# The first quarter of the modulation channel, tile by tile: one layer of a hybrid diffusion backbone on one core

## The chip, the cores and the metric

The kernel runs on one core of one Trainium2 chip. The metric is the device time of one execution in microseconds (us), as the median of several runs. Profiles are of one execution each, taken by the hardware profiler. Engines are named as the profile names them: PE (TensorE; PEld is its weight load), DVE (VectorE), ACT (ScalarE), POOL (GpSimd) and SP (the queue that issues most of the transfers). L12 is line 12 of the kernel.

## The reference, cut to what matters

```python
sh_x, sc_x, gt_x = jnp.split((jax.nn.silu(c) @ w_ada[l] + b_ada[l])[:, None, :], 3, axis=-1)
sh_c, sc_c, gt_c = jnp.split(jax.nn.silu(c_ctx) @ w_ada[l] + b_ada[l], 3, axis=-1)
pc = split_proj(modulate(ctx, sh_c, sc_c), w_in[l], b_in[l])   # h * (1 + scale) + shift, then @ w_in
px = split_proj(modulate(x, sh_x, sc_x), w_in[l], b_in[l])
...                                                            # RG-LRU, differential attention, gMLP
qx = apply_axial_rope(px[2].reshape(B, T, DIFF_HEADS, 2, DIFF_HEAD_DIM), cos, sin)
kx = apply_axial_rope(px[3].reshape(B, T, DIFF_HEADS, 2, DIFF_HEAD_DIM), cos, sin)
kc = pc[3].reshape(B, C, DIFF_HEADS, 2, DIFF_HEAD_DIM)
```

There are 512 latent tokens (x), 256 context tokens (ctx) and 1024 channels; w_ada is 1024 x 3072, w_in 1024 x 12288, all float32. Before anything can be projected, the shift and the scale of every channel must be known: a product of one vector (two of them, for x and for ctx) with two thirds of w_ada.

## The kernel before

The 1024 channels are eight tiles of 128 on the partitions. The head of the kernel (L264 to L457) brings x and ctx from token-major to channel-major, modulates them, and computes the first keys and queries (heads 0 and 1) over the channel tiles as these become ready. It works in four quarters r of two channel tiles each. For quarter 0:

- `to_cm` (L354) transposes x on PE, four 128 x 128 blocks to a channel tile, both tiles of the quarter one after the other.
- `ada_mm` (L332) multiplies the two silu vectors with the quarter's columns of w_ada: for each of 8 row tiles k four products j, each on a 32-column strip of the PE array (`tile_position`), j = 0, 1 for the shift of the two channel tiles, j = 2, 3 for the scale. The compiler makes two PE instructions of each float32 product, so one call is 64 PE instructions. DVE copies the result out of PSUM (adas, L341).
- `ada_cols` (L344) transposes adas on PE (adat), and four DVE instructions add the biases (mods, L351).
- `modulate` (L367) is, for each channel tile, one DVE multiply-add (xm, L372), an ACT copy that rounds to fp32r (the high part, L374) and a subtraction (the low part, L375; on DVE for x, on POOL for ctx).
- `more(name, r)` (L401) adds a quarter's share to a product. `mm3` (L57) makes three PE instructions for each channel tile: high x high (L62), high x low (L63), low x high (L64).

The order of PE is the order of the program, written by hand (`manual_schedule`). The order of DVE, ACT, POOL and SP is chosen by the framework from its own estimate of when each instruction is ready, earlier program lines first. After quarter 0 the loop of L409 runs, on PE: k0, q0, k1, q1 over quarter 0 (24 instructions, 128 x 512), `ada_mm(1)`, kc0, `ada_cols(1)`, and so on for the other quarters, then the values (v).

Transfers go through SP in program order. A weight of w_in for one head (raw, 512 KB, rows of 512 bytes) has three buffers; its rounding is `w_conv` (L118): an ACT copy (L133) and a subtraction (L134) on DVE or POOL. raw 0 is k0's weight, then q0, k1 and q1. The fourth raw needs the buffer of the first. On SP stand, in this order: x of quarter 0 (512 KB, rows of 1 KB), three small rows of vectors, w_ada of quarter 0 (two blocks of 256 columns, shift and scale, in two halves by row tile, 4 x 512 KB, rows of 1 KB), raw 0, raw 1, ctx of quarter 0 (256 KB), x of quarter 1, raw 2, raw 3, w_ada of quarter 1 (2 x 1 MB), and so on.

Of the kernel before, what the change touches and what calls it, by code (L numbers as in the profile page):

```python
# [10 lines left out]
F32 = mybir.dt.float32  # L11
F32R = mybir.dt.float32r  # L12
AF = mybir.ActivationFunctionType
ALU = mybir.AluOpType
PSUM = bass.MemoryType.PSUM

P = 128
D = 1024
KT = 8
T = 512  # L20
TC = 256
# [8 lines left out]
def block_kernel(ctx, tc, x, c, cctx_in, c_ctx, w_ada, b_ada, w_in, b_in, conv_w, conv_b,  # L30
# [3 lines left out]
    nc = tc.nc  # L34
    V, S, G, PE = nc.vector, nc.scalar, nc.gpsimd, nc.tensor
# [11 lines left out]
    def acc_t(name):  # L47
        return acc.tile([P, 512], F32, tag="acc", name=name)

    def big_t(name):  # L50
        return big.tile([P, 1024], F32, tag="big", name=name)
# [5 lines left out]
    def mm3(ps, A, B, asl, bsl, first=True, last=True):  # L57
        n = len(asl)
        for i in range(n):
            ah, al = A[0][asl[i]], A[1][asl[i]]  # L60
            bh, bl = B[0][bsl[i]], B[1][bsl[i]]
            PE.matmul(ps, ah, bh, start=(first and i == 0), stop=False)  # L62
            PE.matmul(ps, ah, bl, start=False, stop=False)  # L63
            PE.matmul(ps, al, bh, start=False, stop=(last and i == n - 1))  # L64

    def proj_cm(ps, W, X, n0, n1, ks=range(KT)):
        mm3(ps, W, X, [np.s_[:, k, :] for k in ks], [np.s_[:, k, n0:n1] for k in ks],
            0 in ks, KT - 1 in ks)
# [13 lines left out]
    reqs, pieces, raws, parts, last = [], [], {}, {}, {}  # L82
# [15 lines left out]
    def w_dma():  # L98
        if state["dma"] >= len(pieces):
            return  # L100
        i, part = pieces[state["dma"]]
        kind, src, c0 = reqs[i][:3]
        if kind == "cm":
            raw = wp.tile([P, KT, P], F32, tag="raw", bufs=3, name=f"raw{i}")
            nc.sync.dma_start(raw, src[:, c0:c0 + P].rearrange("(k p) c -> p k c", p=P))
        elif kind != "tm":
            raw = wp.tile([P, 2, 512], F32, tag="raw", bufs=3, name=f"raw{i}_{part}")
            r0 = 512 * int(kind[1]) + 256 * part
            nc.sync.dma_start(raw, src[r0:r0 + 256, c0:c0 + 512]
                              .rearrange("(k p) c -> p k c", p=P))  # L110
        else:
            raw = wp.tile([P, KT // 2, CW], F32, tag="raw", bufs=3, name=f"raw{i}_{part}")
            nc.sync.dma_start(raw, src[part * 512:part * 512 + 512, c0:c0 + CW]
                              .rearrange("(k p) c -> p k c", p=P))
        raws[state["dma"]] = raw
        state["dma"] += 1
# [54 lines left out]
    for p in range(3):  # L171
        i, ha_, hb_ = 8 * p, 2 * p + 2, 2 * p + 3
# [83 lines left out]
    X = (xh[:, 0], xh[:, 1])  # L256
    chl = gp.tile([P, 2, KT, TC], F32R, tag="c", name="chl")
    C = (chl[:, 0], chl[:, 1])
# [4 lines left out]
    pre = {}  # L263
    with tc.tile_pool(name="hd", bufs=1) as hd:  # L264
        colA = hd.tile([P, P], F32, name="colA")
        mods = hd.tile([P, 4, KT], F32, name="mods")
# [14 lines left out]
        adaw = {}  # L281

        def load_ada(r):
            for c0 in (256 * r, 1024 + 256 * r):
                adaw[c0] = hd.tile([P, KT, 256], F32, tag="ada", bufs=6, name=f"ada{c0}")
            n = KT // 2 if r == 0 else KT
            for k0 in range(0, KT, n):
                for c0 in (256 * r, 1024 + 256 * r):
                    nc.sync.dma_start(adaw[c0][:, k0:k0 + n],
                                      w_ada[0][k0 * P:(k0 + n) * P, c0:c0 + 256]  # L290
                                      .rearrange("(k p) c -> p k c", p=P))

        def load_x(r):
            cs = slice(256 * r, 256 * r + 256)
            nc.sync.dma_start(xtok[:, :, cs], x[0].rearrange("(t p) d -> p t d", p=P)[:, :, cs])

        def load_c(r):
# [1 line left out]
            nc.sync.dma_start(ctok[:, :, cs],  # L299
                              cctx_in[0].rearrange("(t p) d -> p t d", p=P)[:, :, cs])  # L300

        load_x(0)
        load_ada(0)
        w_dma()
        w_dma()
        load_c(0)
        load_x(1)
        w_dma()
# [20 lines left out]

        adas = {}  # L330

        def ada_mm(r):  # L332
            ps = acc_t(f"ada{r}")
            for k in range(KT):
                for j in range(4):
                    c0 = 256 * r + (1024 if j >= 2 else 0)
                    PE.matmul(ps[32 * j:32 * j + 32, 0:P], w32[:, k, :],
                              adaw[c0][:, k, (j % 2) * P:(j % 2) * P + P],
                              start=(k == 0), stop=(k == KT - 1), tile_position=(0, 32 * j))
            sb = hd.tile([P, P], F32, tag="adas", bufs=2, name=f"adas{r}")  # L340
            V.tensor_copy(sb, ps[:, 0:P])  # L341
            adas[r] = sb

        def ada_cols(r):  # L344
            tp = acc_t(f"adat{r}")
            PE.transpose(tp[:, 0:P], adas[r], ident)
            tv = tp[:, 0:P].rearrange("p (t j i) -> p t j i", t=2, j=2)
            for i in range(2):
                for sc in range(2):
                    o = 16 + 8 * sc + 2 * r  # L350
                    V.scalar_tensor_tensor(mods[:, 2 * i + sc, 2 * r:2 * r + 2], tv[:, sc, :, i],  # L351
                                           float(sc), colA[:, o:o + 2], op0=ALU.add, op1=ALU.add)

        def to_cm(r, i):  # L354

            tok, n = ((xtok, T), (ctok, TC))[i]
            tps = [big_t(f"x{i}_0")] if r == 0 else [acc_t(f"x{i}_{r}{j}") for j in range(2 - i)]
            pss = []
            for j in range(2):
                k = 2 * r + j  # L360
                ps = tps[j][:, 0:n] if len(tps) == 2 else tps[0][:, j * n:j * n + n]
                for tt in range(n // P):
                    PE.transpose(ps[:, tt * P:(tt + 1) * P], tok[:, tt, k * P:(k + 1) * P], ident)
                pss.append(ps)
            return pss

        def modulate(r, i, pss):  # L367
            dst, n = ((xh, T), (chl, TC))[i]
            for j in range(2):
                k = 2 * r + j  # L370
                xm = hd.tile([P, n], F32, tag=f"xm{i}", bufs=2, name=f"xm{i}_{k}")
                V.tensor_scalar(xm, pss[j], mods[:, 2 * i + 1, k:k + 1], mods[:, 2 * i, k:k + 1],  # L372
                                op0=ALU.mult, op1=ALU.add)
                S.copy(dst[:, 0, k, :], xm)  # L374
                (V if i == 0 else G).tensor_tensor(dst[:, 1, k, :], xm, f(dst[:, 0, k, :]),  # L375
                                                   ALU.subtract)

        x0 = to_cm(0, 0)
        ada_mm(0)
        ada_cols(0)  # L380
        load_ada(3)
        bi = b_in[0].rearrange("(k p) -> k p", p=P)
        nc.sync.dma_start(rowC[0:96, :], bi)
# [5 lines left out]
        nc.sync.dma_start(rowB[40:56, :], lru_ba[0].rearrange("d (k p) -> (d k) p", p=P))  # L389
        nc.sync.dma_start(rowB[56:72, :], lru_bx[0].rearrange("d (k p) -> (d k) p", p=P))  # L390
        nc.sync.dma_start(rowB[88:96, :], sgu_b[0])
        modulate(0, 0, x0)
        modulate(0, 1, to_cm(0, 1))
        state["use"] = 4

        bks = [big_t(f"pre{i}") for i in range(3)]
        for h in range(2):
            pre["k", h], pre["q", h] = bks[h][:, 0:512], bks[h][:, 512:1024]
            pre["kc", h] = bks[2][:, 512 * h:512 * h + TC]

        def more(name, r):  # L401
            j, h = int(name[-1] == "1") * 2 + int(name[0] == "q"), int(name[-1])
            ks = range(2 * r, 2 * r + 2)
            if name[:2] == "kc":
                proj_cm(pre["kc", h], parts[j], C, 0, TC, ks)
            else:
                proj_cm(pre[name[0], h], parts[j], X, 0, T, ks)

        for r in range(4):  # L409
            more("k0", r)  # L410
            more("q0", r)
            if r == 0:
                state["lo"] = V
                w_conv()
                w_conv()
                state["lo"] = G
                more("k1", r)
                more("q1", r)
            if r == 3:
                more("kc0", r)  # L420
            else:
                ada_mm(r + 1)
            more("kc0" if r == 0 else "k1", r)
            if r < 3:
                ada_cols(r + 1)
                modulate(r + 1, 0, to_cm(r + 1, 0))
            more("kc1" if r == 0 else "q1", r)
            if r < 3:
                modulate(r + 1, 1, to_cm(r + 1, 1))
            if 0 < r < 3:  # L430
                more("kc0", r)
            if r > 0:
                more("kc1", r)
# [20 lines left out]
                               op1=ALU.subtract)  # L454
# [538 lines left out]
    for i in range(9):  # L993
# [3 lines left out]
        if i < 7:  # L997
            W = w_next()
            ps = (acc_t if i else big_t)(f"xa{i + 1}")[:, 0:T]
# [3 lines left out]
            ps = (acc_t if i else big_t)(f"xac{i + 1}")  # L1003
# [121 lines left out]
    for g in range(8):  # L1125
        ps = acc_t(f"gt0{g}")
# [4 lines left out]
        ps = acc_t(f"y0{g}")  # L1131
# [35 lines left out]
    for g in range(8):  # L1167
        ps = acc_t(f"gt2{g}")
# [42 lines left out]
    for g in range(8):  # L1211
        ps = acc_t(f"y2{g}")
# [31 lines left out]
    for half in range(2):  # L1244
        W = w_next()
        for tt in (0, 2, 1, 3):
            ps = bk[tt // 2][:, tt % 2 * 512:tt % 2 * 512 + 512]
# [75 lines left out]
```

## Time and profile before

| | us |
|---|---|
| median of 3 runs | 1012.86 |
| the runs | 1012.6 to 1014.95 |
| the profiled execution, its own time | 1009.53 |
| the span of its profile | 1007.8 |

The profile's views used below are: busy time by stretch (for each stretch its length, then for each engine the busy time and the number of instructions, then the granted clock of PE, the share of the transfer engines and the rate), the timeline of one engine (start, duration or length of a merged group, engine, line, operation, output from inputs; in brackets the idle time before it and what ended it), the chain of work that ended last (start, length, what), and the rate of transfers in slices. Merged groups show the time from the first start to the last end.

### The profile page before, as it was taken

How to read it: one execution, taken by the hardware profiler on the slowest of the kernel's cores; microseconds unless marked ns; L12 is line 12 of the kernel's file. 1: busy time of each engine (PE TensorE's matmuls, PEld its weight loads, DVE VectorE, ACT ScalarE, POOL GpSimd, SP SyncE). 2: the span in 40 equal slices, each digit the busy share in tenths (PEclk: the TensorE clock that was granted, in tenths of full speed). 3: DMA queues.
4: the chain of work that ended last, by engine and by line, in shares of the span. 5: the costliest groups of instructions: out<-in, count | busy, mean ns of one | idle time of the engine just before them, and what ended most of it. 6: DMA issues, size and time to landing. Idle time of an engine off the chain costs nothing.

```text
span 1007.8 us, 13228 instructions
## 1 busy us (share of the span) xinstructions
PE 964.8 (96%) x5239; PEld 816.5 (81%) x5239; DVE 656.2 (65%) x996; ACT 525.7 (52%) x741; POOL 154.8 (15%) x118
## 2 busy tenths in 40 slices
PE   5998899989989999999999999999999999999996
PEld 4796688878878888878888888788888888888886
DVE  4479688787797764788787776378323356425567
ACT  4155846647656797898777886323222133323221
POOL 2143324242342262100000000000000000000002
PEclk7998999989989999999999999999999999999999
DMA  9933130130131122223322323735322432754222
GB/s 309 306 102 89 43 84 22 44 104 21 43 87 39 43 84 63 63 75 93 95 85 83 94 66 112 252 92 154 98 84 84 120 89 73 253 167 144 95 63 84
DMA packets 142996, 103.34 MB, mean 103 GB/s; under 512 B 3629, under 2 KB 133142, under 8 KB 142934
## 3 DMA queue, kind: packets, MB, share of 16 engines
q1 hardware_dynamic: 140790, 95.85, 31.2%
q0 software_dynamic: 2000, 6.56, 2.4%
q8 instruction: 41, 0.67, 0.3%
q14 instruction: 21, 0.17, 0.0%
q10 hardware_dynamic: 144, 0.10, 0.0%
HBM read 94.10 MB, written 4.19 MB: 98 GB/s over the span
## 4 chain that ended last, share of the span: by engine, by line
PE 68%; DVE 17%; ACT 10%; issue 3%; DMA 1%; SPq 1%; POOL 0%; POOLq 0%; ACTq 0%; DVEq 0%
PE y L62 4%; PE y L64 4%; PE y L63 4%; PE gt L62 4%; PE gt L63 4%; PE gt L64 4%; DVE mxn L735 2%; DVE e L750 2%; PE s L725 2%; DVE kd L585 2%; PE out L63 2%; DVE kd L590 1%; PE out L64 1%; PE out L62 1%; PE gc L62 1%
## 5 line engine op out<-in xcount | busy, mean ns | idle before, releaser
L133 ACT CAST w<-raw 128x1024 fp32r<-128x1024 f32 x96 | 99.8, 1045 | 81.9 <-PE y L64 25.3
L134 DVE TENSOR_TENSOR w<-raw,w 128x1024 fp32r<-128x1024 f32 x71 | 86.3, 1220 | 75.4 <-ACT w L133 75.4
L62 PE MATMUL gt<-xhl,w 128*128 128x512 f32 x192 | 75.5, 393 | 0.0
L64 PE MATMUL gt<-xhl,w 128*128 128x512 f32 x192 | 74.8, 390 | 0.0
L63 PE MATMUL gt<-xhl,w 128*128 128x512 f32 x192 | 74.8, 390 | 0.0
L725 PE MATMUL s<-kd,qdq 128*128 128x512 f32 (+1 forms) x256 | 59.0, 371 | 13.1 <-DVE e L750 5.3
L134 POOL TENSOR_TENSOR w<-raw,w 128x1024 fp32r<-128x1024 f32 x25 | 60.9, 2441 | 67.5 <-ACT w L133 67.5
L725 PEld LDWEIGHTS s<-kd,qdq 128*128 128x128 f32 x256 | 44.8, 198 | 24.7 <-issue 12.2
L735 DVE TENSOR_REDUCE mxn<-s 128x1 f32<-128x768 f32 x64 | 58.3, 949 | 8.2 <-PE s L725 8.2
L740 ACT ACTIVATE e<-s,mxn 128x768 f32<-128x768 f32 x32 | 28.8, 900 | 48.5 <-DVE mxn L735 48.5
L1204 POOL PARTITION_BROADCAST grb<-grs x8 | 3.8, 581 | 297.7 <-DVE grs L1201 297.7
L62 PEld LDWEIGHTS gt<-xhl,w 128*128 128x128 f32 x192 | 36.1, 188 | 7.7
L64 PEld LDWEIGHTS gt<-xhl,w 128*128 128x128 f32 x192 | 36.0, 188 | 7.7
L63 PEld LDWEIGHTS gt<-xhl,w 128*128 128x128 f32 x192 | 36.1, 188 | 7.0
L967 POOL DMA_DIRECT2D pa_d<-ha x8 | 4.4, 552 | 220.4 <-DVE ha L966 220.4
L750 DVE SCALAR_TENSOR_TENSOR e<-s,sm,e 128x768 f32<-128x768 f32 x32 | 32.5, 1017 | 6.5 <-ACT e L743 5.7
L54 ACT CAST vh<-v 128x128 fp32r<-128x128 f32 x48 | 12.4, 263 | 42.9 <-PE v L64 19.7
L862 ACT ACT_TABLE_LOAD x25 | 32.1, 1283 | 0.4
L768 DVE TENSOR_TENSOR wtl<-t,wth 128x768 fp32r<-128x768 f32 x32 | 30.3, 949 | 0.6 <-ACT wth L766 0.5
L743 ACT ACTIVATE e<-e,sm 128x768 f32<-128x768 f32 x32 | 29.9, 935 | 0.2 <-DVE sm L742 0.2
L862 ACT ACTIVATE rt<-ri,colB 128x770 f32<-128x770 f32 x32 | 28.1, 904 | 2.5 <-PE ri L64 1.4
L740 ACT ACTIVATE s<-s,mxn 128x768 f32<-128x768 f32 x32 | 27.7, 865 | 0.9 <-DVE mxn L735 0.9
(458 smaller groups left out, 3037.6 us busy)
## 6 DMA issues: line engine op xcount, KB each, us to landing
raw<-in_w_in_dram SPq DMA_DIRECT2D x96, 512.0 KB, 4.0
raw<-in_w_branch_dram SPq DMA_DIRECT2D x24, 512.0 KB, 4.1
ada<-in_w_ada_dram SPq DMA_DIRECT2D x6, 1024.0 KB, 8.5
qdq<-qdq POOLq DMA_DIRECT2D x16, 256.0 KB, 3.2
adg<-in_w_ada_dram SPq DMA_DIRECT2D x8, 512.0 KB, 5.9
raw<-in_w_out_dram SPq DMA_DIRECT2D x8, 512.0 KB, 3.6
xtok<-in_x_dram SPq DMA_DIRECT2D x4, 512.0 KB, 5.6
ada<-in_w_ada_dram SPq DMA_DIRECT2D x4, 512.0 KB, 5.7
```

The source lines that it names most:

```text
L62: PE.matmul(ps, ah, bh, start=(first and i == 0), stop=False)
L63: PE.matmul(ps, ah, bl, start=False, stop=False)
L64: PE.matmul(ps, al, bh, start=False, stop=(last and i == n - 1))
L133: state["hi"] = S.copy(h, raws[j])
L134: state["lo"].tensor_tensor(l, raws[j], f(h), ALU.subtract)
L725: PE.matmul(sp[:, sl], qds[h][:, 2 * m + j, qs], kds[h][:, m, sl], start=(j == 0), stop=(j == 1))
L735: V.tensor_reduce(mxn[:, m:m + 1], sps[m][:, 0:TA], mybir.AxisListType.X, ALU.max, negate=True)
L740: S.activation(e, sps[m][:, 0:TA], AF.Exp, bias=mxn[:, m:m + 1], accum_out=sm[:, m:m + 1])
L743: S.mul(es[i][0], es[i][0], sm[:, 0:1])
L750: V.scalar_tensor_tensor(e0, e1, sm[:, 1:2], e0, op0=ALU.mult, op1=ALU.add)
L768: V.tensor_tensor(wts[h][1][:, :, qs], src, f(wts[h][0][:, :, qs]), ALU.subtract)
L862: order[0] = S.activation(out, in_, fn, **kw)
```

## The change

The w_ada blocks of quarter 0 are loaded in halves by column (128 columns of shift and scale: one channel tile) and no longer in halves by row tile, and x of quarter 0 in two halves of 128 channels. On SP stand now: x of tile 0, w_ada of tile 0, raw 0, x of tile 1, w_ada of tile 1, raw 1, and then everything as before. The pieces have rows of 512 bytes. `ada_mm(0)` and `ada_cols(0)` are called twice, for j = (0, 2) and j = (1, 3); each call of the half makes 32 PE instructions on two strips of the array, a memset and two 32-partition copies in place of one copy, one PE transpose and four small DVE additions. `modulate` of x is called for tile 0, then the three PE instructions of k0 over tile 0 follow, then the second half; the loop's first k0 is cut to tile 1. The two transposed tiles of x of quarter 0 have a PSUM buffer each; `to_cm` still transposes both before the first `ada_mm`.

```diff
         def load_ada(r):
...
-            n = KT // 2 if r == 0 else KT
-            for k0 in range(0, KT, n):
+            for j in range(2 if r == 0 else 1):
+                n = 128 if r == 0 else 256
+                cs = slice(128 * j, 128 * j + n)
+                if r == 0:
+                    load_x(0, cs)
                 for c0 in (256 * r, 1024 + 256 * r):
-                    nc.sync.dma_start(adaw[c0][:, k0:k0 + n],
-                                      w_ada[0][k0 * P:(k0 + n) * P, c0:c0 + 256]
+                    nc.sync.dma_start(adaw[c0][:, :, cs],
+                                      w_ada[0][:, c0 + 128 * j:c0 + 128 * j + n]
                                       .rearrange("(k p) c -> p k c", p=P))
+                if r == 0:
+                    w_dma()
...
-        load_x(0)
         load_ada(0)
-        w_dma()
-        w_dma()
         load_c(0)
...
-        def ada_mm(r):
-            ps = acc_t(f"ada{r}")
+        def ada_mm(r, js=range(4)):
+            ps = acc_t(f"ada{r}_{js[0]}")
             for k in range(KT):
-                for j in range(4):
+                for j in js:
...
-            sb = hd.tile([P, P], F32, tag="adas", bufs=2, name=f"adas{r}")
-            V.tensor_copy(sb, ps[:, 0:P])
+            sb = hd.tile([P, P], F32, tag="adas", bufs=2, name=f"adas{r}_{js[0]}")
+            if len(js) == 4:
+                V.tensor_copy(sb, ps[:, 0:P])
+            else:
+                V.memset(sb, 0.0)
+                for j in js:
+                    V.tensor_copy(sb[32 * j:32 * j + 32, :], ps[32 * j:32 * j + 32, 0:P])
...
-            tps = [big_t(f"x{i}_0")] if r == 0 else [acc_t(f"x{i}_{r}{j}") for j in range(2 - i)]
+            tps = [(big_t if r + i == 0 else acc_t)(f"x{i}_{r}{j}") for j in range(2 - i)]
...
         x0 = to_cm(0, 0)
-        ada_mm(0)
-        ada_cols(0)
...
+        for j in range(2):
+            ada_mm(0, (j, j + 2))
+            ada_cols(0, j, 1)
+            modulate(0, 0, x0, (j,))
+            if j == 0:
+                more("k0", 0, (0,))
...
-        modulate(0, 0, x0)
         modulate(0, 1, to_cm(0, 1))
...
         for r in range(4):
-            more("k0", r)
+            more("k0", r, (1,) if r == 0 else None)
             more("q0", r)
```

## Rows read from the trace of the kernel before

**Rows 1.** The page: busy time, share of the span, instructions.
```profile
PE 964.8 (96%) x5239; PEld 816.5 (81%) x5239; DVE 656.2 (65%) x996; ACT 525.7 (52%) x741; POOL 154.8 (15%) x118
```
**Rows 2.** Busy time by stretch; the last three columns are PE's clock, transfer share, GB/s.
```profile
10.00:13.00 3.00, 1.69 (x41) 1.07 (x34) 0.29 (x1) 0.17 (x1) 0.00 (x0) 1.00 1.14 344
13.00:24.00 11.00, 7.78 (x19) 5.49 (x20) 8.79 (x13) 5.99 (x8) 4.44 (x3) 0.53 1.07 344
24.00:60.00 36.00, 35.42 (x356) 29.11 (x355) 15.34 (x39) 8.36 (x15) 4.32 (x6) 1.00 0.71 226
...
78.00:85.00 7.00, 5.46 (x25) 5.49 (x26) 6.67 (x14) 2.79 (x6) 2.81 (x3) 0.54 0.33 77
```
**Rows 3.** Timeline of PE from the first transposes to quarter 1.
```profile
7.80 2.74 PE L337 MATMUL ada<-ada,w 128*32 128x128 f32 x36
11.46 1.07 PE L337 MATMUL ada<-ada,w 128*32 128x128 f32 x28 [0.92 <-DMA ada<-in_w_ada_dram]
...
15.06 1.11 PE L363 MATMUL x<-ident,ctok 128*128 128x128 f32 x4 [1.81 <-DMA ctok<-in_ctx_dram]
16.69 0.79 PE L62 MATMUL pre<-xhl,w 128*128 128x512 f32 x1 [0.51 <-ACT xhl L374]
18.38 0.80 PE L63 MATMUL pre<-xhl,w 128*128 128x512 f32 x1 [0.90 <-DVE xhl L375]
...
26.41 1.95 PE L337 MATMUL ada<-ada,w 128*32 128x128 f32 x64
...
29.11 0.27 PE L346 MATMUL adat<-ident,adas 128*128 128x128 f32 x1
...
32.10 0.50 PE L63 MATMUL pre<-xhl,w 128*128 128x512 f32 x1 [0.16 <-DVE xhl L375]
```
**Rows 4.** Timeline of DVE in the same stretch.
```profile
12.57 0.29 DVE L341 COPY adas<-ada 128x128 f32<-128x128 f32 x1 [5.34 <-PE ada L337]
13.90 1.22 DVE L134 TENSOR_TENSOR w<-raw,w 128x1024 fp32r<-128x1024 f32 x1 [0.39 <-ACT w L133]
...
15.18 1.52 DVE L372 TENSOR_SCALAR xm<-x,mods 128x512 f32<-128x512 f32 x2
16.66 1.65 DVE L375 TENSOR_TENSOR xhl<-xm,xhl 128x512 fp32r<-128x512 f32 x1
...
28.43 0.29 DVE L341 COPY adas<-ada 128x128 f32<-128x128 f32 x1 [5.65 <-PE ada L337]
...
31.36 0.69 DVE L375 TENSOR_TENSOR xhl<-xm,xhl 128x512 fp32r<-128x512 f32 x1
```
**Rows 5.** Timelines of ACT (first two rows) and of POOL.
```profile
12.82 1.04 ACT L133 CAST w<-raw 128x1024 fp32r<-128x1024 f32 x1 [4.78 <-DMA raw<-in_w_in_dram]
14.28 1.04 ACT L133 CAST w<-raw 128x1024 fp32r<-128x1024 f32 x1 [0.41 <-DMA raw<-in_w_in_dram]
...
15.41 2.36 POOL L134 TENSOR_TENSOR w<-raw,w 128x1024 fp32r<-128x1024 f32 x1 [13.90 <-ACT w L133]
```
**Rows 6.** Transfer rate of the first 60 us, 40 slices of 1.5 us each.
```profile
GB/s 0 200 206 321 378 358 344 348 350 358 358 315 275 386 363 352 355 347 348 348 348 350 379 382 350 353 351 348 331 122 8 209 350 143 9 0 0 0 0 0
```
**Rows 7.** The chain that ended last: product instructions at two clocks, end of the head.
```profile
20.45 0.43 PE pre L64
...
24.41 0.23 PE pre L62
...
57.60 1.06 ACT w4h L133
...
59.82 1.23 DVE w4l L134
...
61.52 1.78 SPq L491
63.36 4.15 DMA rops<-in_rope_s_dram
67.60 1.26 DVE t1k L544
```

More of the change, by code (lines that the diff above doesn't have):

```diff
@@ L285, in load_ada, with load_x @@
                 adaw[c0] = hd.tile([P, KT, 256], F32, tag="ada", bufs=6, name=f"ada{c0}")
-            n = KT // 2 if r == 0 else KT
-            for k0 in range(0, KT, n):
+            for j in range(2 if r == 0 else 1):
[3 more added lines that the diff above has]
+                    load_x(0, cs)
                 for c0 in (256 * r, 1024 + 256 * r):
-                    nc.sync.dma_start(adaw[c0][:, k0:k0 + n],
-                                      w_ada[0][k0 * P:(k0 + n) * P, c0:c0 + 256]
+                    nc.sync.dma_start(adaw[c0][:, :, cs],
+                                      w_ada[0][:, c0 + 128 * j:c0 + 128 * j + n]
                                       .rearrange("(k p) c -> p k c", p=P))
-        def load_x(r):
-            cs = slice(256 * r, 256 * r + 256)
+                if r == 0:
+                    w_dma()
+        def load_x(r, cs=None):
+            if cs is None:
+                cs = slice(256 * r, 256 * r + 256)
             nc.sync.dma_start(xtok[:, :, cs], x[0].rearrange("(t p) d -> p t d", p=P)[:, :, cs])
@@ L339, in ada_mm, with ada_cols @@
                               start=(k == 0), stop=(k == KT - 1), tile_position=(0, 32 * j))
-            sb = hd.tile([P, P], F32, tag="adas", bufs=2, name=f"adas{r}")
-            V.tensor_copy(sb, ps[:, 0:P])
+            sb = hd.tile([P, P], F32, tag="adas", bufs=2, name=f"adas{r}_{js[0]}")
[5 more added lines that the diff above has]
+                    V.tensor_copy(sb[32 * j:32 * j + 32, :], ps[32 * j:32 * j + 32, 0:P])
             adas[r] = sb
-        def ada_cols(r):
-            tp = acc_t(f"adat{r}")
+        def ada_cols(r, j0=0, n=2):
+            tp = acc_t(f"adat{r}_{j0}")
             PE.transpose(tp[:, 0:P], adas[r], ident)
@@ L349, in ada_cols @@
                 for sc in range(2):
-                    o = 16 + 8 * sc + 2 * r
-                    V.scalar_tensor_tensor(mods[:, 2 * i + sc, 2 * r:2 * r + 2], tv[:, sc, :, i],
-                                           float(sc), colA[:, o:o + 2], op0=ALU.add, op1=ALU.add)
+                    k = 2 * r + j0
+                    o = 16 + 8 * sc + k
+                    V.scalar_tensor_tensor(mods[:, 2 * i + sc, k:k + n], tv[:, sc, j0:j0 + n, i],
+                                           float(sc), colA[:, o:o + n], op0=ALU.add, op1=ALU.add)
         def to_cm(r, i):
             tok, n = ((xtok, T), (ctok, TC))[i]
-            tps = [big_t(f"x{i}_0")] if r == 0 else [acc_t(f"x{i}_{r}{j}") for j in range(2 - i)]
+            tps = [(big_t if r + i == 0 else acc_t)(f"x{i}_{r}{j}") for j in range(2 - i)]
             pss = []
@@ L365, in to_cm, with modulate @@
             return pss
-        def modulate(r, i, pss):
+        def modulate(r, i, pss, js=range(2)):
             dst, n = ((xh, T), (chl, TC))[i]
-            for j in range(2):
+            for j in js:
                 k = 2 * r + j
@@ L378, in block_kernel, with more @@
         x0 = to_cm(0, 0)
-        ada_mm(0)
-        ada_cols(0)
+        bks = [big_t(f"pre{i}") for i in range(3)]
+        for h in range(2):
+            pre["k", h], pre["q", h] = bks[h][:, 0:512], bks[h][:, 512:1024]
+            pre["kc", h] = bks[2][:, 512 * h:512 * h + TC]
+        def more(name, r, ks=None):
+            j, h = int(name[-1] == "1") * 2 + int(name[0] == "q"), int(name[-1])
+            ks = ks or range(2 * r, 2 * r + 2)
+            if name[:2] == "kc":
+                proj_cm(pre["kc", h], parts[j], C, 0, TC, ks)
+            else:
+                proj_cm(pre[name[0], h], parts[j], X, 0, T, ks)
+        for j in range(2):
[4 more added lines that the diff above has]
+                more("k0", 0, (0,))
         load_ada(3)
@@ L391, in block_kernel @@
         nc.sync.dma_start(rowB[88:96, :], sgu_b[0])
-        modulate(0, 0, x0)
         modulate(0, 1, to_cm(0, 1))
         state["use"] = 4
[L396 to L407, printed above, removed]
         for r in range(4):
-            more("k0", r)
+            more("k0", r, (1,) if r == 0 else None)
             more("q0", r)
```

## Prediction

> **What bounds the kernel now.** The page's busy times come first [rows 1]: PE is busy 964.8 of 1007.8 us, so a gain in another engine counts only where PE waits for it. The stretches [rows 2] show where it does near the change: from 13 to 24 us PE is busy 7.78 of 11 us at a granted clock of 0.53, that is, nearly all of it at the lower level of 1.2 GHz, and from 24 to 60 us it is busy 35.42 of 36 us at full clock. So the head is paced by transfers and the modulation chain up to about 18 us, and by PE from there to 60. The timelines [rows 3, 4] give the chain: the last w_ada half lands at 11.46, the product ends at 12.53, DVE copies it, PE transposes it, then xm at 15.18, the rounding on ACT, the low part at 16.66, and the first product that needs a low part starts at 18.38. From there PE runs to `ada_mm(1)` at 26.41 with no wait.
>
> What a shift there is worth at the end is read from the chain that ended last [rows 7]: the first rounding of the v weight at 57.60 follows the last quarter's products, the rope tables are issued on SP behind it (61.52), land, and release DVE at 67.60. Every link is timed from PE's end of the head, none from a fixed hour. I therefore count each microsecond by which `ada_mm(1)` moves as one microsecond of the total.
>
> **When the pieces land.** The rate in slices [rows 6] sums to 2.19 MB at 9.0 us, 2.71 at 10.5 and 3.23 at 12. As a test of the method: x and w_ada of quarter 0 with raw 0 are 3.17 MB, which have passed at 11.8, and raw 0's rounding, which waits for that transfer, starts at 12.82 [rows 5]; the lag is 1.0. In the new order tile 1's x is complete after 0.26 + 0.02 + 1.05 + 0.52 + 0.26 = 2.12 MB: passed at 8.8, landed at 9.9. Tile 1's w_ada is complete after 3.17 MB: landed at 12.8, so 1.4 us later than the last w_ada half now, because raw 0 has gone ahead of it. raw 1 stays at 14.3, as the bytes before it are the same. I take the rows of 512 bytes at the old rate: the slices from 10.5 to 15, in which raw 0 and raw 1 pass with such rows, show 344 to 358 GB/s, and those before, with rows of 1 KB, 321 to 378. Were the pieces moved at 344 instead of 358, 2.6 MB would cost 0.3 us.
>
> The other end is fixed too. w_ada of quarter 1 is complete after 7.62 MB, which the slices reach at 24.7; landed at about 25.75. `ada_mm(1)` starts at 26.41 now. **However early the products of quarter 0 come, at most 0.7 us can be won**, since PE's next step waits for that transfer.
>
> **The change part by part.** Removed is the wait of the first product for tile 1's w_ada and for the second xm. Moved are three of the 24 products of k0 to q1. Added is a second pass of adas, adat, mods, and PE has to take it in order. I follow PE through its new program.
>
> (1) Both tiles of x are still transposed ahead of the first `ada_mm`, so this now waits for tile 1's x (9.9), though its own w_ada has landed at about 7.7. Four transposes took 1.11 at the lower clock (ctok) [rows 3]: 11.0.
>
> (2) The half `ada_mm` has 32 instructions on two strips. The whole one took 1.95 for 64 [rows 3], 16 groups of four on four strips, 0.12 a group. No row shows two strips. If the instructions of a strip follow each other and the strips run beside each other, the half has 16 groups as well and costs the full 1.95 at 2.4 GHz, twice that (3.9) at 1.2 GHz. If the instructions are issued one by one at 1.95 / 64 = 0.03 us, it costs 0.98 (1.95 at the lower clock). I take the first reading, since 0.12 is near half of the 0.23 that a product of 512 columns at one pass each takes [rows 7], as 128 columns at two cycles each would. By clock the ends are 0.98 and 3.9. Today's call ran 36 instructions in 2.74 and 28 in 1.07 [rows 3], with one wait between, so partly at the lower level; I take 2.9 for the first half (half the groups at each level): 13.9.
>
> The Trainium skill, page "TensorEngine Tiling (Array Packing)", section "Theoretical Speedup", gives up to 4x for a small dimension of 32 and up to 2x for 64. Two used strips of 32 columns would by that table get 2x at most, so half the work takes the same time, which is the reading taken; no row here shows it.
>
> (3) From the end of `ada_mm` to the product that needs the low part: in quarter 1 from 28.36 to 32.10, 3.74, of which adat stood 0.39 behind other products (adas ends 28.72, adat starts 29.11) [rows 3, 4]. One copy more adds 0.29: 3.6. The memsets go into DVE's idle time before. The low part of tile 0 starts at about 16.8, beside POOL's 2.36 us on the q0 weight, which now starts at 15.41 and hangs on raw 1 as before [rows 5]; the same subtraction beside it took 1.65 against 0.69 alone [rows 4]. I add 0.95: 18.4. At nothing it would be 17.5.
>
> (4) Tile 0's last two products at 0.43 [rows 7]: 19.3. Only now may PE start the second `ada_mm`, whose w_ada has lain there since 12.8. This is the price of putting a product that waits for DVE between the two halves. Second half as the first, 2.9 (again 0.98 to 3.9): 22.2. Chain again 3.6: 25.8. raw 1's rounding and POOL are then past; the k1 and q1 weights' subtractions (1.22 each on DVE) may stand in the way, priced below.
>
> (5) From 25.8, 20 of the 24 products remain. At the higher clock they take 20 x 0.23 = 4.7, at the lower 8.6. Now the clock fell in the gaps before 18.38 and rose only after some 5 us of products without a gap (23 products took 8.03, 0.43 each and then 0.23). With PE idle about 3.5 us ahead of them again, I take 6.5: 32.3.
>
> **Sum.** `ada_mm(1)` starts at 32.3 instead of 26.41: +5.9. With the second half at 3.9 it would be 6.9; with the first two lower bounds of the chain (no POOL contention, higher clock in both halves, 4.7 for the products) 9.9 + 1.1 + 1.95 + 3.6 + 0.9 + 1.95 + 3.6 + 4.7 = 27.7, +1.3. I forecast **+6**. Against the profiled execution (1009.53, span 1007.8) that is 1015.5; the median before is 3.3 higher, 1012.86, so I predict 1018.9. One extra issue on SP (x in two pieces) costs nothing, as transfers there are limited by rate and not by issue. A difference of 0.3%, 3.0 us, is about what a measurement of this kernel can tell from no change.
>
> **The rivals.**
> *Halves at half the price (0.22).* PE issues the strips' instructions one by one and stays at the higher clock: 9.9 + 0.55 + 0.98 + 3.6 + 0.5 + 0.98 + 3.6 = 20.1, then 6.5: 26.6, +0.2, between -0.7 and +3: 1013, within 0.3%. It decides if the group time with two strips falls below about 0.08. For it: no row shows two strips. Against it: PE is idle more than now, and at 1.2 GHz even this reading costs 1.95.
> *Faster (0.04).* The early product fills the gap, PE reaches w_ada of quarter 1 at 25.75 (-0.7), and in addition the later stretch at the lower clock (5.46 us busy at 0.54, 78 to 85 us) [rows 2] falls away, which gives 5.46 / 2 = 2.7: -3.4, 1009.5. Nothing in the change touches that stretch but the hour at which PE arrives.
> *More in the chain (0.16).* The framework already put a 1.22 us weight subtraction (13.90) between PE's transpose and xm [rows 4]. With two chains there are two places for it, and an ACT rounding of 1.04 [rows 5] may stand ahead of xh's: +1.2 to +2.4 on the sum, 1020 to 1021.5. If `ada_mm` for tile 0 waits for both column halves after all (that is, the split does nothing), it starts at 12.8 and not 11.0, +1.8, the same range.
> *Transfers (in the last case's chance).* The Trainium skill, page "DMA: Bandwidth & Descriptors", section "Rules for kernel authors", asks for few transfers of 1 MiB or more, and its fit has about 2.0 us fixed for each; x in two pieces would then bring tile 1's x 2 us later. In the rows such a price doesn't show: with pieces of 256 and 512 KB in the queue the slices stay at 344 to 358 [rows 6].
>
> **How the numbers follow.** The forecast (+3 to +8.5, chance 0.58) and the longer chain (0.16) are slower by over 0.3%: 0.74. Same: 0.22. Faster: 0.04. The likeliest case's own range is 1016 to 1021.5. The range that leaves out two in ten goes lower into the case of cheap halves: 1012.8 to 1021.8.
>
> **What would show it.** Right: the first x transposes of tile 1 near 10 us; 32 L337 instructions taking about 2 us at the higher or 3.9 at the lower clock; the second `ada_mm` starting only after the first k0 products, near 19; two gaps of some 3.5 us on PE between 13 and 26; `ada_mm(1)` near 32; the same order and lengths from there on, shifted. Wrong: a half call of 1 us; the granted clock at 1.00 through 13 to 24; `ada_mm(1)` waiting for its transfer at 25.8; or the shift shrinking between 32 and 75 us.

## The result and the profile after

The changed kernel takes 1021.93 us (median of 4 runs, 1019.81 to 1022.73), the kernel before 1012.73 beside it: a ratio of 1.0087, 95% interval 1.0073 to 1.0101, so **9.2 us slower**. The direction and the mechanism are those of the prediction; the size, forecast as +6, came out half as large again: 1021.93 is 0.1 us above the upper end of the stated range, 1021.8. The profiled execution took 1022.73 (span 1020.8), which is 0.8 over its median, where that of before was 3.3 under its own; so the two traces differ by 13.2, and the medians by 9.2.

The timeline of PE after (columns as before) answers to [rows 3]. The two passes over the chain are to be seen in it:

```profile
10.93 1.11 PE L372 MATMUL x<-ident,xtok 128*128 128x128 f32 x4 [5.58 <-DMA xtok<-in_x_dram]
13.12 3.63 PE L340 MATMUL ada<-ada,w 128*32 128x128 f32 x32 [1.08 <-DVE w L331]
17.43 0.33 PE L354 MATMUL adat<-ident,adas 128*128 128x128 f32 x1 [0.68 <-DVE adas L349]
...
20.30 0.79 PE L63 MATMUL pre<-xhl,w 128*128 128x512 f32 x1 [0.23 <-DVE xhl L384]
...
21.45 2.91 PE L340 MATMUL ada<-ada,w 128*32 128x128 f32 x32
25.17 0.30 PE L354 MATMUL adat<-ident,adas 128*128 128x128 f32 x1 [0.82 <-DVE adas L349]
...
29.28 0.50 PE L63 MATMUL pre<-xhl,w 128*128 128x512 f32 x1 [1.49 <-DVE xhl L384]
...
35.65 1.95 PE L340 MATMUL ada<-ada,w 128*32 128x128 f32 x64
```

PE waits 5.6 us for tile 1's x, then 1.1 for w32, the silu vectors. The first half of the product ends at 16.75, the first low part is used at 20.30, and the second half follows the three products at 21.45. `ada_mm(1)` starts at 35.65, where before it started at 26.41 [rows 3]: **+9.24 us, the whole loss, is there at this instruction.** From it on the order is that of before, and PE's instructions stay later by 8.7 to 10.2 us up to 122 us of before. Between 122 and 132 us the shift rises to 12.5, and it ends at 13.1. That step does not depend on how late a kernel is: the run with the loads only (below), which costs 0.4 us, has it against the trace of before too (0.45 to 3.1), that with halves in quarters 1 to 3, later by 6.35 us there, does not. As the profiled execution of before was 3.3 us under its median, the step is likely that execution's own; what makes it is not shown. The rows of the chain that ended last, after, answer to [rows 7]:

```profile
66.84 1.07 ACT w4h L133
...
69.08 1.23 DVE w4l L134
...
70.78 0.73 SPq L504
71.57 6.11 DMA rops<-in_rope_s_dram
77.77 1.23 DVE t1k L557
```

The rounding of the v weight comes 9.24 us later (66.84 for 57.60) and DVE's first step behind the rope table 10.17 later, as this transfer took 6.11 for 4.15.

The timelines of DVE and (last four rows) ACT after, which answer to [rows 4, 5], show what stood in the way that the prediction had not placed:

```profile
16.79 0.58 DVE L349 COPY adas<-ada 32x128 f32<-32x128 f32 x2 [3.73 <-PE ada L340]
...
19.55 0.69 DVE L384 TENSOR_TENSOR xhl<-xm,xhl 128x512 fp32r<-128x512 f32 x1 [0.69 <-ACT xhl L383]
24.43 0.59 DVE L349 COPY adas<-ada 32x128 f32<-32x128 f32 x2 [4.19 <-PE ada L340]
...
25.78 1.71 DVE L381 TENSOR_SCALAR xm<-x,mods 128x512 f32<-128x512 f32 x3
27.40 1.22 DVE L134 TENSOR_TENSOR w<-raw,w 128x1024 fp32r<-128x1024 f32 x1
28.53 0.69 DVE L384 TENSOR_TENSOR xhl<-xm,xhl 128x512 fp32r<-128x512 f32 x1
...
10.00 1.05 ACT L133 CAST w<-raw 128x1024 fp32r<-128x1024 f32 x1 [7.99 <-DMA raw<-in_w_in_dram]
...
11.06 1.28 ACT L328 ACT_TABLE_LOAD   x1
12.36 0.22 ACT L328 ACTIVATE sg<-colA 128x16 f32<-128x16 f32 x1
...
15.67 1.05 ACT L133 CAST w<-raw 128x1024 fp32r<-128x1024 f32 x1 [1.80 <-DMA raw<-in_w_in_dram]
```

ACT now rounds raw 0's weight before it takes the sigmoid from which w32 is made: the input of the sigmoid (colA) is there at 4.8, but ACT, idle for 8 us until raw 0 arrives, takes the sigmoid only at 12.36. Behind the rounding stands a table load of 1.28 us (an instruction that ACT runs ahead of the sigmoid), which before was over long in advance:

```profile
2.01 1.28 ACT L325 ACT_TABLE_LOAD   x1
6.53 0.22 ACT L325 ACTIVATE sg<-colA 128x16 f32<-128x16 f32 x1 [3.23 <-DVE colA L323]
```

And DVE subtracts the k1 weight (27.40) between tile 1's xm and its low part (28.53).

### The profile page after: what moved, and what is told of

The parts are those of the page before. It is cut to its first block, busy times and chain, and to the rows that moved or that the text cites. A ratio compares the mean times of both kernels' runs of the same rounds, so it can differ in the third digit from the quotient of the medians.

```text
span 1020.8 us, 13239 instructions
## 1 busy us (share of the span) xinstructions
PE 966.7 (95%) x5240; PEld 817.5 (80%) x5240; DVE 659.3 (65%) x1005; ACT 525.9 (52%) x741; POOL 157.0 (15%) x118
## 4 chain that ended last, share of the span: by engine, by line
PE 67%; DVE 17%; ACT 10%; issue 3%; DMA 2%; SPq 0%; POOL 0%; POOLq 0%; ACTq 0%; DVEq 0%
PE y L62 4%; PE y L64 4%; PE y L63 4%; PE gt L64 4%; PE gt L62 4%; PE gt L63 4%; DVE mxn L748 2%; DVE e L763 2%; DVE kd L598 2%; PE s L738 2%; PE out L63 1%; DVE kd L603 1%; PE out L64 1%; PE out L62 1%; PE gc L62 1%
## 5 line engine op out<-in xcount | busy, mean ns | idle before, releaser
L738 PEld LDWEIGHTS s<-kd,qdq 128*128 128x128 f32 x256 | 44.2, 195 | 28.3 <-issue 15.1
```

The lines of the kernel that those rows point to most:

```text
L738: PE.matmul(sp[:, sl], qds[h][:, 2 * m + j, qs], kds[h][:, m, sl], start=(j == 0), stop=(j == 1))
```

## The experiments

The theory: the loss is one serial chain on PE, in which the second half of the product stands behind three products that wait for the whole modulation chain of tile 0. The rivals: the new loads themselves (later pieces, short rows); the half calls as such; single waits on ACT and DVE. All runs below are whole kernels; "over before" is the median against that of the kernel before on the same chip, beside it the ratio of the two with its interval. The column "head" is how much later than in the trace of before PE reaches the first transpose that follows the head (tcolB, 60.81 there); it and the start of `ada_mm(1)` come from one profiled execution each, the totals are medians.

| kernel | ada_mm(1) starts | head | over before | ratio |
|---|---|---|---|---|
| before | 26.41 | 0 | 0 | |
| changed | 35.65 | +9.3 | +9.2 | 1.0087 (1.0073 to 1.0101) |
| halves in quarters 1 to 3 | 28.34 | +5.9 | +4.6 | 1.0047 (1.0028 to 1.0066) |
| loads only | 27.50 | +1.1 | +0.4 | 1.0006 (0.9995 to 1.0017) |
| halves only | 35.73 | +9.3 | +9.5 | 1.0088 (1.0069 to 1.0106) |
| no product between | 29.00 | +2.6 | +4.1 | 1.0035 (1.0023 to 1.0047) |
| sigmoid first | 34.49 | +8.1 | +7.9 | 1.0080 (1.0061 to 1.0100) |
| and tile 1's x behind | 34.38 | +8.0 | +7.3 | 1.0072 (1.0048 to 1.0097) |
| and no product between | 27.89 | +1.5 | +1.2 | 1.0015 (1.0002 to 1.0028) |
| tile 1's x behind, rounding on DVE | 29.69 | +3.3 | +2.1 | 1.0016 (1.0003 to 1.0029) |
| halves only, together | 28.04 | +1.6 | +1.3 | 1.0015 (1.0005 to 1.0025) |

Over all ten changed kernels the total follows the head within about 1.5 us.

**What a half call costs, and whether a delay reaches the end.** The kernel before, with the calls of quarters 1 to 3 in two halves, back to back:

```diff
-            for k in range(KT):
-                for j in range(4):
+            for js in ((range(4),) if r == 0 else ((0, 2), (1, 3))):
+              for k in range(KT):
+                for j in js:
```

> The kernel before, with ada_mm of quarters 1, 2 and 3 issued as two calls of 32 instructions on two strips, back to back, into the same PSUM tile and with the one copy; quarter 0, loads and everything else stay. PE runs at the higher clock there, without waits. If the instructions of one strip follow each other, each half costs as much as the whole (1.95 us), so ada_mm of each of these quarters takes 3.8 us and the total rises by 3 x 1.9 = 5.7 us. If instructions are issued one by one at 0.03 us, each half costs 0.98 and the total stays where it is (0). A rise of 5.7 us in the total would also show that a delay of PE in the head reaches the end undiminished.

Its PE timeline, quarter 1's call and quarter 2's (before: 1.95 and 1.96 for the same 64):

```profile
28.34 3.28 PE L338 MATMUL ada<-ada,w 128*32 128x128 f32 x62 [1.65 <-DMA ada<-in_w_ada_dram]
...
38.44 3.29 PE L338 MATMUL ada<-ada,w 128*32 128x128 f32 x64
```

1.34 us more for each call, between the two readings and nearer to that of full price. The starts of the single instructions in the traces show why: the instructions of one group start 7 ns apart on their strips, and the groups follow each other at 0.11 us, with two strips here as with four before. So a half has as many steps as the whole. Where the two halves meet, some groups of the second start beside those of the first, which saves a part; alone, and with its groups 0.11 us apart too, a half took 1.94 for 32 instructions (below), as long as the whole call of 64. The total rose by 4.6, 3 x 1.34 = 4.0 of it by the calls. In this execution PE also waited 1.65 us for w_ada of quarter 1, which landed at 28.3.

**Loads or computation.** First the changed loads with the computation of before:

```diff
-        for j in range(2):
-            ada_mm(0, (j, j + 2))
-            ada_cols(0, j, 1)
-            modulate(0, 0, x0, (j,))
-            if j == 0:
-                more("k0", 0, (0,))
+        ada_mm(0)
+        ada_cols(0)
+        modulate(0, 0, x0)
...
-            more("k0", r, (1,) if r == 0 else None)
+            more("k0", r)
```

> The changed kernel's loads (column halves, raw 0 ahead of tile 1) with the computation of before: one ada_mm(0) of 64 instructions, one ada_cols, both tiles modulated together, k0 over both tiles. If the serial chain of PE is what costs, most of the 9.2 us are gone: ada_mm(0) waits for tile 1's w_ada (about 14, against 11.5 before), so ada_mm(1) starts near 29 and the total is 2 to 4 us over before. If it is the loads themselves, the total stays 7 to 9 us over before.

Then the reverse, the loads of before with the changed computation (`load_ada(0)` in halves by row tile, x in one piece ahead of it, both raws behind it):

> The loads of the kernel before (x in one piece, w_ada halves by row tile, raw 0 and raw 1 behind) with the changed kernel's computation: two half calls of ada_mm(0), two chains, three products of k0 between. If the serial chain costs: first half ends near 13, low part of tile 0 near 17.5, second half starts near 19 although its w_ada landed at 11.5, ada_mm(1) near 32 to 33, total 5 to 7 us over before. If it is the loads, the total is within 2 us of before.

PE timelines of the loads alone (first two rows) and of the halves alone:

```profile
14.16 3.23 PE L340 MATMUL ada<-ada,w 128*32 128x128 f32 x58 [0.67 <-DMA ada<-in_w_ada_dram]
...
20.64 0.79 PE L63 MATMUL pre<-xhl,w 128*128 128x512 f32 x1 [0.20 <-DVE xhl L384]
```
```profile
20.33 3.39 PE L338 MATMUL ada<-ada,w 128*32 128x128 f32 x32
24.54 0.30 PE L352 MATMUL adat<-ident,adas 128*128 128x128 f32 x1 [0.82 <-DVE adas L347]
...
28.64 0.80 PE L63 MATMUL pre<-xhl,w 128*128 128x512 f32 x1 [1.26 <-DVE xhl L382]
```

The loads alone cost next to nothing, less than I had expected (2 to 4): w_ada is 2.7 us later (14.16 for 11.46), but raw 0 ahead of it takes the 1.22 us weight subtraction and POOL's stretch out of the chain, so the first low part is used at 20.64 for 18.38. Of these 2.3 us half is won back by the clock: the 23 products from there to `ada_mm(1)` take 6.86 for 8.03, since fewer of them run at the lower level. The halves alone bring the whole loss, 9.5, more than expected (5 to 7). There w_ada of both tiles has landed by 11.8, and the second half still starts at 20.33. **The changed computation, not the loads, is what costs.**

**The product between.**

```diff
             modulate(0, 0, x0, (j,))
-            if j == 0:
-                more("k0", 0, (0,))
...
-            more("k0", r, (1,) if r == 0 else None)
+            more("k0", r)
```

> The changed kernel without the product between: the second half of ada_mm(0) follows the first transpose of adas at once, and k0 over both tiles follows both. If the three products between the halves hold the second half back, it starts near 17.8 in place of 21.45 and the total falls by 3 to 4 us against the changed kernel (5 to 6 over before). If something else does (transfers, DVE), it stays within 1 us of the changed kernel.

```profile
17.10 1.94 PE L340 MATMUL ada<-ada,w 128*32 128x128 f32 x32
...
24.24 0.50 PE L63 MATMUL pre<-xhl,w 128*128 128x512 f32 x1 [1.49 <-DVE xhl L384]
...
29.00 1.96 PE L340 MATMUL ada<-ada,w 128*32 128x128 f32 x64
```

`ada_mm(1)` comes 6.65 us earlier than in the changed kernel, and the total falls by 5.0, more than the 3 to 4 expected. 4.35 is the start of the second half (17.10 for 21.45). The rest is the clock: the half takes 1.94 for 2.91, and the 20 products that remain 4.76 for 6.37; the wait between them is 0.3 longer. The granted clock of the changed kernel (first fence: busy time by stretch, as in [rows 2]) and of this one (second):

```profile
20.00:24.00 4.00, 3.77 (x33) 2.79 (x34) 0.24 (x1) 1.51 (x2) 0.00 (x0) 0.57 1.09 366
24.00:30.00 6.00, 2.32 (x17) 1.44 (x12) 5.07 (x12) 1.31 (x3) 2.38 (x1) 1.00 1.10 349
30.00:34.00 4.00, 4.00 (x13) 3.09 (x12) 0.36 (x1) 0.00 (x0) 1.64 (x2) 0.57 1.10 349
```
```profile
20.00:24.00 4.00, 1.80 (x9) 1.05 (x8) 3.97 (x10) 2.26 (x4) 1.42 (x1) 1.00 1.10 368
24.00:30.00 6.00, 5.76 (x56) 4.68 (x60) 1.32 (x2) 0.00 (x0) 2.61 (x2) 1.00 1.11 349
```

The changed kernel's PE stands idle for 3.7 of 6 us from 24 to 30 and then runs 30 to 34 mostly at 1.2 GHz; the other is at 2.4 GHz throughout. The same edit on the loads of before:

> The loads of the kernel before with two half calls of ada_mm(0) and two chains, but no product between the halves. All w_ada lands at 11.5 here, so the halves run one after the other. If the product between is what made the run with halves only 9.5 us slower, ada_mm(1) starts near 28 and the total is 1 to 3 us over before; if it is the two half calls and two chains as such, it stays above 6.

```profile
14.44 3.63 PE L338 MATMUL ada<-ada,w 128*32 128x128 f32 x32
...
28.04 1.96 PE L338 MATMUL ada<-ada,w 128*32 128x128 f32 x64
```

1.3 over before, against 9.5 with the product between: 8.2 of the 9.5 hang on those three products, as expected. The second half took 3.63 here, the length of the lower level, so leaving out the product does not by itself bring the half the higher one.

**The single waits.** The sigmoid is written ahead of the weight roundings (the lines from tcolA to w32 moved in front of the first `w_conv`):

> The changed kernel with the sigmoid of the vectors ahead of the first weight rounding on ACT (the rounding is written behind it, so the framework cannot put a rounding that waits for raw 0 in front). The first half of ada_mm no longer waits for w32 (13.1) but only for tile 1's x and its transposes: start near 12.0. The same change takes the k1 weight's subtraction out of the way between xm and the low part of tile 1. If both count, the total falls by 1.1 + 1.2 = 2.3 us against the changed kernel (7 over before); if other waits take their place, by under 1.

Two rows of PE and one of DVE:

```profile
11.75 3.23 PE L340 MATMUL ada<-ada,w 128*32 128x128 f32 x32
...
20.79 3.63 PE L340 MATMUL ada<-ada,w 128*32 128x128 f32 x32
...
17.79 1.79 DVE L384 TENSOR_TENSOR xhl<-xm,xhl 128x512 fp32r<-128x512 f32 x1 [0.68 <-ACT xhl L383]
```

The first half started at 11.75 (13.12), and nothing stood between tile 1's xm and its low part; but tile 0's low part now fell beside POOL's subtraction and took 1.79, and the second half ran at 1.2 GHz throughout (3.63). 1.3 won, not 2.3. Next, tile 1's x is transposed behind the first half:

```diff
-        x0 = to_cm(0, 0)
+        x0 = to_cm(0, 0, (0,))
...
             ada_mm(0, (j, j + 2))
+            if j == 0:
+                to_cm(0, 0, (1,), x0)
```

> As the run with the sigmoid first, and the transposes of tile 1's x moved behind the first half of ada_mm, so that PE no longer waits for tile 1's x (10.9) ahead of tile 0's products. The first half starts when tile 0's w_ada has landed, near 8 to 8.5, the first k0 product comes near 16, and the second half starts near 17 (21.45 in the changed kernel). If the wait for x is on the path, the total is 3 to 4 us under the run with the sigmoid first (about 3.5 us over before). If the second half, held back by the products between, is what sets the time, it shrinks less, to 5 or 6 over before.

Timelines of PE, DVE, ACT and POOL in this kernel:

```profile
8.13 3.40 PE L340 MATMUL ada<-ada,w 128*32 128x128 f32 x30 [1.00 <-DMA ada<-in_w_ada_dram]
...
20.62 3.63 PE L340 MATMUL ada<-ada,w 128*32 128x128 f32 x32
...
13.02 0.80 DVE L384 TENSOR_SCALAR xm<-x,mods 128x512 f32<-128x512 f32 x1
16.99 2.43 DVE L387 TENSOR_TENSOR xhl<-xm,xhl 128x512 fp32r<-128x512 f32 x1 [3.17 <-ACT xhl L386]
...
15.39 1.04 ACT L133 CAST w<-raw 128x1024 fp32r<-128x1024 f32 x1 [3.52 <-DMA raw<-in_w_in_dram]
16.34 0.61 ACT L386 CAST xhl<-xm 128x512 fp32r<-128x512 f32 x1
...
16.52 2.35 POOL L134 TENSOR_TENSOR w<-raw,w 128x1024 fp32r<-128x1024 f32 x1 [15.00 <-ACT w L133]
```

The first half starts 3.6 us earlier than with the sigmoid first (all but two of its instructions, which come at 6.53), and the second half at 20.62 for 20.79: all of it is given back, and the total, 7.3 over before, is above both values expected. xm is done at 13.82, but on ACT the q0 weight's rounding stands in front of xh's and waits for raw 1 until 15.39; then the low part runs beside POOL's subtraction (16.52 to 18.87) and takes 2.43 instead of 0.69. Whether this order on ACT is the cause was tested by rounding tile 0's high part on DVE:

```diff
-                S.copy(dst[:, 0, k, :], xm)
+                if r + i + j == 0:
+                    V.tensor_copy(dst[:, 0, k, :], xm)
+                else:
+                    S.copy(dst[:, 0, k, :], xm)
```

> As the run with tile 1's x behind, and the high part of tile 0's x rounded on DVE, not on ACT, where the rounding of the q0 weight stands ahead of it and waits for raw 1 (15.3). If that order on ACT gave back what moving x had won, the low part of tile 0 is ready near 15 (19.4 in the run before), the second half starts near 16.2 (20.6), and ada_mm(1) near 29 to 30 (34.4): the total falls by 4 to 5 us, to about 3 over before. If something else sets the start of the second half, it stays at 6 to 7 over.

```profile
15.46 0.50 PE L63 MATMUL pre<-xhl,w 128*128 128x512 f32 x1 [0.16 <-DVE xhl L390]
...
16.13 3.09 PE L340 MATMUL ada<-ada,w 128*32 128x128 f32 x32
...
14.71 0.69 DVE L390 TENSOR_TENSOR xhl<-xm,xhl 128x512 fp32r<-128x512 f32 x1
```

It is: the low part is used at 15.46 (19.47 with x behind), the second half starts at 16.13, and of 7.3 over before 2.1 are left, with the product still between. Two things go together here: ACT's wait, and the stretch beside POOL, ahead of whose subtraction the low part (14.71) now comes. The last run takes the other way, sigmoid first, x behind and no product between:

> The changed loads with all three serial steps undone: sigmoid first, tile 1's x transposed behind the first half, and no product between the halves. The second half then starts when tile 1's w_ada lands (14.2), the low part of tile 1 comes near 20.5, ada_mm(1) near 26.5 to 27.5, as in the kernel before (26.4), since w_ada of quarter 1 lands near 26 in either. Total within 1.5 us of before. If the half calls by themselves cost more than that (1.3 us each over a half of the whole call), 2 to 3 us over.

```profile
14.02 3.62 PE L340 MATMUL ada<-ada,w 128*32 128x128 f32 x30 [0.37 <-DMA ada<-in_w_ada_dram]
...
27.89 1.95 PE L340 MATMUL ada<-ada,w 128*32 128x128 f32 x64
```

The second half now waits for its own w_ada, and 1.2 is left. No version tried is faster than the kernel before.

## Why the prediction was right, and where it was too small

**What bounds the head, and 1:1 to the end: right.** The shift of `ada_mm(1)` was 9.24, that of the total 9.2; the table shows the same for ten kernels, within about 1.5 us, and the shift did not shrink on the way (9.25 at tcolB).

**The sum, step by step.** Predicted and measured, each in us:

| step | predicted | measured |
|---|---|---|
| (landing) tile 1's x landed | 9.9 | 10.9 |
| (1) to the start of the first half | 1.1 | 2.2 |
| (2) first half | 2.9 | 3.6 |
| (3) to the low part of tile 0 | 4.55 | 3.55 |
| (4) two products | 0.9 | 1.15 |
| (4) second half | 2.9 | 2.9 |
| (4) to the low part of tile 1 | 3.6 | 4.9 |
| (5) 20 products | 6.5 | 6.4 |
| ada_mm(1) starts | 32.3 | 35.65 |

The steps themselves all appear, in the order given. The likeliest case, +3 to +8.5, does not hold 9.2, nor does the longer chain as it was priced (1020 to 1021.5); that the total still lies at the edge of the range is owed to errors of both signs. Four terms were mis-sized. *The landing*: I kept the old rate for the new pieces; see the last section. (The slices from 10.5 to 15 that I read for rows of 512 bytes show 348 to 358, not 344.) 2.12 MB had passed at 9.5 instead of 8.8, so the rate makes 0.7 of the 1.0; the rival of 2 us for a further transfer does not show. Tile 1's w_ada and raw 1 were late as well (14.0 to 14.2 in two of the runs for 12.8, and 15.67 for 14.3). *Step (1)*, +1.1: I had the sigmoid and w32 ready, as they are in the trace of before, and didn't ask what raw 0's earlier place does to ACT's order. The framework puts what it takes to be ready first, and ACT then waits for the transfer with the sigmoid and its table load behind it. In the prediction's own terms this is the rival of more in the chain, with the ACT rounding in front of another instruction than the one I named. *Step (2)*, +0.7: the first half ran wholly at the length of the lower clock; 3.6 is what 32 instructions take there, near the upper bound (3.9). *Step (4)*, +1.3: the weight subtraction in the second chain, which stood among that rival's prices (+1.2). Against them stands -1.0 in *step (3)*: POOL's subtraction had ended when tile 0's low part came, because everything was later than I had placed it. *Step (5)* is right in its number by luck: I had the first products at the lower level and the rest at the higher, but the clock was at 1.00 from 24 to 30 us, fell behind PE's idle time, to 0.57 from 30 to 34, and rose again.

**The half calls: right.** At the higher clock the half took 1.94, the whole 1.95; at the lower 3.63. The groups follow each other at the same 0.11 us on two strips as on four, which is the first of the two readings. The rival of halves at half the price is refuted by the run with halves in quarters 1 to 3 (1.34 more a call, not 0).

**"This is the price of putting a product that waits for DVE between the two halves": right and the main cause.** Taking it out is worth 8.2 of 9.5 with the old loads, 5.0 of 9.2 with the new ones, and 6.1 of 7.3 there once the sigmoid and tile 1's x are out of the way. Its price isn't fixed: it is the time by which tile 0's chain outlasts what else the second half waits for (its w_ada, the end of the first half), and what the clock adds. With that chain shortened (sigmoid first, tile 1's x behind, rounding on DVE) only 2.1 of the loss remained with the product in place.

**Tile 1's x ahead of the first `ada_mm`: real, but not worth what step (1) suggests.** Moving it won 3.6 us at the first half and nothing at the second, since ACT's wait for raw 1 was next in line. I had priced the steps as a sum; some of them cover each other.

**At most 0.7 us can be won: neither shown nor refuted by its number.** One run did end up waiting for w_ada of quarter 1, as said, but at 28.3 and not 25.75 (halves in quarters 1 to 3). Its loads are those of before, where the same transfer had landed by 26.41; so the bound's kind is right and its place moves between executions by more than the 0.7.

## What to carry to other kernels

On an engine that runs in the written order, an early piece of work that waits for other engines holds back everything written behind it, ready or not: put the independent half first, and the dependent product behind it. When a transfer is moved forward, look at every in-order queue on which its consumer then stands ahead of something older. And before a product on four strips of the array is cut into two on two strips, read whether the instructions of one strip are what takes the time; if so, each half costs nearly the whole.

## What the runs showed of the hardware

**Rate of short rows.** The transfer rates of the first 60 us after, in slices of 1.5 us, answer to [rows 6]:

```profile
GB/s 0 164 177 322 294 338 339 289 302 361 380 349 349 384 365 353 349 350 349 347 348 347 373 363 376 349 347 348 347 236 24 17 257 353 85 0 0 11 0 0
```

From 6 to 13.5 us they are 289 to 339, where before they were 344 to 378; by 13.5 us 3.34 MB have passed instead of 3.76, 1.2 us' worth. The Trainium skill, page "DMA: Bandwidth & Descriptors", section "Specifications", has 512 bytes as the least transfer for the full rate; the pieces have just that and run slower than those of 1 KB, though raw 0 and raw 1, with rows of 512 bytes too, ran at 348 to 358 before. The run with the loads only has the same dip (293 to 338). An estimate by the bytes in the order of the queue puts raw 0 and tile 1's x into the slices from 7.5 to 10.5 (338, 339) and hardly anything but w_ada's column pieces into those from 10.5 to 13.5 (289, 302). Whether the row length does it or two column pieces of the same rows side by side was not tried.

**DVE beside POOL.** The same DVE subtraction took 0.69 alone and 1.65, 1.79 and 2.43 where it began beside POOL's weight subtraction, and each time ended about half a microsecond after it. The Trainium skill, page "SBUF — State Buffer", section "SBUF: two separate sides", calls the port pair that the two share an exclusive lock for a whole instruction; the rows agree.

**The clock's column at the start.** The changed kernel's view by stretch gives 1.00 from 0 to 20 us, but its first half product took 3.63 there, as long as the second half did in the kernel with x behind, where the column says 0.50 (15 to 24 us). So the level at the beginning is read from the lengths of the instructions. My 2.9 for the first half put half of its groups at the higher level, as the call of before ended there (28 instructions in 1.07); here the groups stayed 0.21 us apart to the end. The sign of being wrong that I had named, a clock of 1.00 through 13 to 24, shows in the column up to 20 us; the lengths refute it up to 16.75, where the first half ends.
